# The first layer's down products with tokens standing and channels moving, summed by tokens and turned by VectorE

## The chip, the cores and the metric

The kernel runs on one core of one Trainium2 chip. The metric is the device time of one execution in microseconds (us). The engines of the core are named as in the profile: PE (TensorE, matmuls), PEld (its weight loads), DVE (VectorE), ACT (ScalarE), POOL (GpSimd) and SP (SyncE, which here only issues DMAs). A matmul has a standing operand of 128x128, loaded into the array ahead of it, and a moving one of up to 512 columns that streams past; its sums are kept in PSUM, 8 banks of 128x512 float32.

## The reference

One layer of a decoder trunk over 512 tokens of 1024 channels, all float32: a half-step SwiGLU feed-forward layer, a mixer (a linear recurrence beside sliding-window attention), and a second feed-forward layer. The change touches the first feed-forward layer and the border to the mixer:

```python
def swiglu(x, w_gu, w_down):
    gate, up = jnp.split(x @ w_gu, 2, axis=-1)
    return (jax.nn.silu(gate) * up) @ w_down

x = x + 0.5 * rms_norm(swiglu(rms_norm(x, ffn1_pre_g[l]), ffn1_w_gu[l], ffn1_w_down[l]), ffn1_post_g[l])
y = hybrid_mixer(rms_norm(x, mix_pre_g[l]), w_in[l], ...)
```

The hidden width is 2816, which is 22 chunks of 128. The product with `w_down` (2816 x 1024) is the "down product"; the kernel calls its result y.

## The kernel before

**Precision.** Every float32 operand is split into a high part, rounded by ACT, and a low part, the difference, made by DVE. A product is three matmuls: high by high, high by low, low by high.

**Groups.** The first layer works through its 22 hidden chunks in groups (`GROUPS1`): 0 to 4 ("classic" products), then three groups of four and a last one of six. In groups 1 to 4 `octo` makes four hidden chunks with a seven-product scheme for 2x2 blocks of matrices (seven "forms" in place of eight block products); its result comes out by tokens, is turned by DVE in blocks of 32x32 (`turned`, line 961), written to HBM by four DMAs (line 965) and read back turned (line 1021, or line 1035 in the last group). While `octo` of one group runs, `seven_forms_of` fetches the group before and makes the seven forms of its hidden values, and `seven_down` then does that group's down product, again with seven forms. So the down products of groups 1, 2 and 3 go through `seven_down`; those of group 0 and of the last group are plain.

**The down products.** They come out with channels on the partitions, as the border to the mixer needs them. In `by_channels` (lines 1339 to 1347) a 128x128 block of `w_down` stands and half of the tokens, 256 columns, move: 24 matmuls a form. The plain products (`product`, lines 506 to 508) let a block of `w_down` stand and all 512 tokens move.

**Sums of the groups.** Partial sums of y are kept in HBM (`in_hbm`, shown as yp_a). Group 0 writes them (line 1416), and each form of `seven_down` that finishes a block is copied out of PSUM by ACT (line 1113) and added to HBM by accumulating DMAs from POOL's queue (line 1116). At the end SP reads y's eight parts back, one for each chunk c of 128 channels (`parts[c]`, lines 1380 and 1389).

**The end of the layer.** The last group's hidden chunks 16 to 19 come from `octo`, 20 and 21 from `quad` (line 881 is its matmul line, in 7 forms). Then eight plain products over six chunks follow, c = 0 to 7, the first two together. For c = 0 to 4 `Residual.chunk` (line 676) adds the product to `parts[c]` on DVE; ACT squares it, and POOL adds up the squares. The last three (`LATE`) go through `boundary`, in two halves of tokens: the products of the first half, `late` on DVE (line 692), squares on ACT, sums on DVE (lines 705, 709); then PE forms the mean square (`stats`, line 550), ACT and DVE invert its root (lines 556 to 560), PE spreads it (line 564), DVE scales y and adds it to x (lines 713, 717), ACT rounds the mixer's input (line 580), and only then can PE begin the mixer's first products (lines 524 and 525).

**What sets the order.** The schedule is manual: each engine, and each DMA queue, runs its instructions in the order in which the program is written. `Weights` feeds the weights. `load` has SP issue the next raw tile (one of five buffers, tag "raw"), `take` and `fill` keep up to four units rounded (ACT) and split (DVE) ahead of the product. When the last unit of a raw tile is split, the next load is issued; if `W.owed` holds something, that is run in the load's place. x itself, two of the five raw buffers, is lent to HBM during the layer (`lend`) and read back (`give_back`, line 1357, POOL's queue) when c = 3.

Of the kernel before, what the change touches and what calls it, by code (L numbers as in the profile page):

```python
# [15 lines left out]
P = 128  # L16
# [106 lines left out]
def tile_layer(ctx: ExitStack, tc: tile.TileContext, out: bass.AP, **ins: bass.AP):  # L123
# [671 lines left out]
    def like(t, x):  # L795

        return t.rearrange("p (a b) -> p a b", a=2) if len(x.shape) == 3 else t

    class Hidden:


        def __init__(self, name, nxt):
            self.name, self.nxt, self.hs, self.g, self.u = name, nxt, {}, {}, {}

# [12 lines left out]
        def split(self, f):  # L817
            us, n = self.u.pop(f), f"{self.name}{f}"
            hh, hl = (spare.pop(), spare.pop()) if spare else (t2k(f"hh{n}", F32R), t2k(f"hl{n}", F32R))
            act.copy(hh, us)  # L820
            dve.tensor_sub(hl, us, hh.bitcast(F32))
            self.hs[f] = (hh, hl)

        def high(self, name, x):

            hh = t2k(f"hh{name}", F32R)
            act.copy(like(hh, x), x)
            self.forms[name] = hh, x

        def low(self, name):  # L830
# [3 lines left out]
            dve.tensor_sub(like(hl, x), x, like(hh.bitcast(F32), x))  # L834
# [171 lines left out]
        def seven_forms_of(self, f, h_hbm, at=(1, 2.5, 3.5, 4.5, 5.5, 6)):  # L1006
# [3 lines left out]
            def fetch():  # L1010
# [6 lines left out]
                z = wide(f"hx{self.name}{f}")  # L1017
                for s in range(2):
# [69 lines left out]
    def seven_down(hid, f, one, part, forms, ahead, beside={}, keep=False):  # L1088
# [7 lines left out]
        for n, (banks, form, blocks) in enumerate(((A, "a11", []), (Dd, "s3", [(1, 1)]), (B, "a12", [(0, 0)]), (A, "s2", [(1, 0)]),  # L1096
# [10 lines left out]
            for i in range(2 if form in (("s3", "s2") if keep else ("a12", "s3", "s2", "s4", "a22", "s1")) else 0):  # L1107
# [6 lines left out]
                for half, dh in blocks:  # L1114
                    o = part(half, dh, i)
                    pool.dma_start(o, st.rearrange("p (a b) -> p a b", a=2) if len(o.shape) == 3 else st, accum_op=ALU.add)  # L1116
# [203 lines left out]
    def masks():  # L1320
# [8 lines left out]
        dve.tensor_copy(up8f, upf)  # L1329
        return neg  # L1330
# [3 lines left out]
    in_hbm = [hbm.tile([P, 2, 2, T // 2], F32, name=f"yp_a{i}") for i in range(KD // 2)]  # L1334

    def in_halves(t):
        return t.rearrange("p (a b) -> p a b", a=2)

    def by_channels(banks, w, h, first):

        (hi, lo), (hh, hl_) = w, h
        for m in range(4):
            o, ms = banks[m // 2][:, HALF[m % 2]], slice(m * P, (m + 1) * P)
            for k in range(2):
                js = HALF[k]
                for i, (a, x) in enumerate(((hi, hh), (hi, hl_), (lo, hh))):
                    pe.matmul(o, a[:, k, ms], x[:, js], start=first and i + k + m % 2 == 0, stop=k == 1 and i == 2, skip_group_check=True)  # L1347
# [697 lines left out]
```

## Time and profile before

| | |
|---|---|
| three timed runs, median (lowest to highest) | 843.85 us (842.74 to 844.1) |
| the profiled execution, its own time | 842.55 us |
| its span in the trace, first to last instruction | 840.8 us |
| granted TensorE clock, mean | 0.999 |
| bytes moved by DMA over the span | 143.73 MB, mean 171 GB/s |
| accumulating DMAs of the first layer from POOL's queue (line 1116) | 42, of 256 KB each |

The stages that the change touches, by the trace (PE is busy through all of them):

| from, to (us) | on PE | DVE busy | DMA share |
|---|---|---|---|
| 58 to 78 | down products of group 0 | 19.20 of 20 | 0.82 |
| 116 to 292 | `octo` and `seven_down`, three times | 161.47 of 176 | 0.59, 0.79, 0.79 |
| 292 to 312 | `quad` | 13.87 of 20 | 1.09 |
| 312 to 332 | plain products c = 0 to 4 of the last group | 10.12 of 20 | 1.01 |
| 332 to 342 | late products, first half and on | 6.37 of 10 | 0.68 |
| 342 to 362 | border: norm, and the mixer's first products | 18.84 of 20 | 0.19 |

How to read the rows: times are us from the start of the span. A timeline row has the start, the time, the engine and line, the operation as out<-in, and in brackets how long the engine had been idle and what ended that. "SPq" is SP's DMA queue: its rows give the time that SP took to issue, not the time until the data have landed. "DMA share" is the mean busy share of the 16 DMA engines; queueing can take it above 1. Matmuls overlap, so one that "takes" 0.28 us can follow the last by 0.12; the chain of waits gives the time by which each one moves the end.

### The profile page before, as it was taken

How to read it: one execution, taken by the hardware profiler on the slowest of the kernel's cores; microseconds unless marked ns; L12 is line 12 of the kernel's file. 1: busy time of each engine (PE TensorE's matmuls, PEld its weight loads, DVE VectorE, ACT ScalarE, POOL GpSimd, SP SyncE). 2: the span in 40 equal slices, each digit the busy share in tenths (PEclk: the TensorE clock that was granted, in tenths of full speed). 3: DMA queues.
4: the chain of work that ended last, by engine and by line, in shares of the span. 5: the costliest groups of instructions: out<-in, count | busy, mean ns of one | idle time of the engine just before them, and what ended most of it. 6: DMA issues, size and time to landing. Idle time of an engine off the chain costs nothing.

```text
span 840.8 us, 12378 instructions
## 1 busy us (share of the span) xinstructions
PE 832.2 (99%) x4504; PEld 718.9 (85%) x4504; DVE 723.8 (86%) x1026; ACT 520.9 (62%) x821; POOL 162.6 (19%) x178
## 2 busy tenths in 40 slices
PE   9999999999999999999999999999999999999996
PEld 8988888988988998987788899888888888888885
DVE  4978999998989965879889589799999899898996
ACT  6646756666666655556797456536758667666562
POOL 2023000140320333304531052002004114032001
PEclk9999999999999999999999999999999999999999
DMA  7249429398595799323511131169439939769842
GB/s 252 77 128 347 135 79 318 80 251 267 123 255 186 167 261 331 93 62 108 157 51 51 51 105 47 50 129 290 179 106 232 317 92 257 253 149 258 305 140 101
DMA packets 123614, 143.73 MB, mean 171 GB/s; under 512 B 23897, under 2 KB 81569, under 8 KB 123041
## 3 DMA queue, kind: packets, MB, share of 16 engines
q1 hardware_dynamic: 109232, 111.86, 42.0%
q0 software_dynamic: 14176, 30.94, 17.0%
q8 instruction: 35, 0.57, 0.3%
q14 instruction: 27, 0.21, 0.1%
q10 hardware_dynamic: 144, 0.13, 0.0%
HBM read 100.45 MB, written 40.89 MB: 168 GB/s over the span
## 4 chain that ended last, share of the span: by engine, by line
PE 96%; DVE 2%; DMA 1%; SPq 0%; issue 0%; ACT 0%; DVEq 0%; ACTq 0%
PE aa L951 10%; PE ab L951 10%; PE db L951 5%; PE da L951 5%; PE yaa L1347 3%; PE bb L951 3%; PE ba L951 3%; PE yda L1347 2%; PE ya L506 2%; PE ya L507 2%; PE ya L508 2%; PE aa L881 1%; PE a_first L1206 1%; PE yab L1884 1%; PE yab L1885 1%; PE yab L1886 1%
## 5 line engine op out<-in xcount | busy, mean ns | idle before, releaser
L1116 POOL DMA_DIRECT2D yp_a<-stage x42 | 36.8, 1064 | 182.6 <-ACT stage L1113 158.8
L1116 POOL DMA_DIRECT2D yp_b<-stage x42 | 36.4, 1084 | 144.3 <-ACT stage L1113 117.8
L506 PE MATMUL ya<-hha,whi_ad 128*128 128x512 f32 x62 | 24.1, 389 | 0.0
L507 PE MATMUL ya<-hla,whi_ad 128*128 128x512 f32 x62 | 24.1, 389 | 0.0
L508 PE MATMUL ya<-hha,wlo_ad 128*128 128x512 f32 x62 | 24.1, 389 | 0.0
L686 POOL TENSOR_TENSOR acca_r<-acca_r,sq_r 128x512 f32<-128x512 f32 x6 | 8.1, 1357 | 61.7 <-ACT sq_r L536 61.7
L1900 POOL DMA_DIRECT2D yp_b<-stage x8 | 4.3, 548 | 67.1 <-ACT stage L1899 67.1
L524 PE MATMUL an<-xh_mx,whi_xl 128*128 128x256 f32 x64 | 15.9, 289 | 0.0
L525 PE MATMUL an<-xh_mx,wlo_xl 128*128 128x256 f32 x64 | 15.5, 283 | 0.0
L2003 POOL TENSOR_TENSOR last<-yp,grow 128x512 f32<-128x512 f32 x3 | 3.9, 1290 | 57.2 <-DVE yp L1993 57.2
L2000 ACT ACTIVATE ysq<-yp 128x512 f32<-128x512 f32 (+1 forms) x8 | 4.8, 606 | 16.2 <-DVE yp L1993 16.2
L506 PE MATMUL gt<-xh_mx,whi_gt 128*128 128x512 f32 x32 | 14.3, 445 | 0.0
L508 PEld LDWEIGHTS ya<-hha,wlo_ad 128*128 128x128 f32 x62 | 11.6, 188 | 2.4
L506 PEld LDWEIGHTS ya<-hha,whi_ad 128*128 128x128 f32 x62 | 11.6, 188 | 2.4
L507 PEld LDWEIGHTS ya<-hla,whi_ad 128*128 128x128 f32 x62 | 11.6, 188 | 2.4
L536 ACT ACTIVATE sq_r<-yp_a 128x256 f32<-128x256 f32 (+1 forms) x10 | 5.0, 502 | 12.9 <-DVE yp_a L676 5.9
L506 PE MATMUL pq<-xh_mx,whi_q 128*128 128x512 f32 x32 | 12.8, 399 | 0.0
L506 PE MATMUL pub<-xh_f,whi_bu 128*128 128x512 f32 x32 | 12.6, 395 | 0.0
L508 PE MATMUL gt<-xh_mx,wlo_gt 128*128 128x512 f32 x32 | 12.6, 394 | 0.0
L506 PE MATMUL pgb<-xh_f,whi_bg 128*128 128x512 f32 x32 | 12.6, 393 | 0.0
L507 PE MATMUL gt<-xl_mx,whi_gt 128*128 128x512 f32 x32 | 12.6, 392 | 0.0
L508 PE MATMUL pgb<-xh_f,wlo_bg 128*128 128x512 f32 x32 | 12.5, 390 | 0.0
(2014 smaller groups left out, 3468.8 us busy)
## 6 DMA issues: line engine op xcount, KB each, us to landing
yp_a<-stage POOLq DMA_DIRECT2D x50, 256.0 KB, 9.1
yp_b<-stage POOLq DMA_DIRECT2D x50, 256.0 KB, 9.0
h_a<-za SPq DMA_DIRECT2D x16, 256.0 KB
hxa<-h_a SPq DMA_DIRECT2D x16, 256.0 KB
h_b<-zb SPq DMA_DIRECT2D x16, 256.0 KB
hxb<-h_b SPq DMA_DIRECT2D x16, 256.0 KB
xn<-in_x SPq DMA_DIRECT2D x8, 256.0 KB
xT_hbm<-xT POOLq DMA_DIRECT2D x2, 1024.0 KB, 9.8
```

The source lines that it names most:

```text
L506: pe.matmul(ps, hi[:, k, :], xh, start=start, stop=False)
L507: pe.matmul(ps, hi[:, k, :], xl, start=False, stop=False)
L508: pe.matmul(ps, lo[:, k, :], xh, start=False, stop=stop)
L524: pe.matmul(ps[:, sl], hi[:, k, :], xh, start=k == 0 and not goes_on, stop=False, skip_group_check=True)
L525: pe.matmul(ps[:, sl], lo[:, k, :], xh, start=False, stop=False, skip_group_check=True)
L881: pe.matmul(o, w[:, k, js], x, start=first and i + j + k == 0, stop=k == 3 and i == 2, skip_group_check=True)
L951: pe.matmul(b[tb], x[:, blk], w[:, k, :], start=first and q + k + j == 0, stop=q + k == 2 and j == 2, skip_group_check=True)
L1116: pool.dma_start(o, st.rearrange("p (a b) -> p a b", a=2) if len(o.shape) == 3 else st, accum_op=ALU.add)
L1206: pe.matmul(banks[j][:, HALF[0]], ws[j][part][:, k, :], n1.xs[k][xpart][:, HALF[0]], start=k == 0 and part == xpart, stop=stop and k == KD ...
L1347: pe.matmul(o, a[:, k, ms], x[:, js], start=first and i + k + m % 2 == 0, stop=k == 1 and i == 2, skip_group_check=True)
L1884: pe.matmul(banks[i], hh[:, js], hi[:, k, :], start=first and k == 0, stop=False, skip_group_check=True)
L1885: pe.matmul(banks[i], hh[:, js], lo[:, k, :], start=False, stop=False, skip_group_check=True)
```

## The change

**Group 0.** Its `w_down` comes in two loads of 512 channels instead of four of 256. `first_down` computes y by tokens: a 128x128 block of the hidden values stands, 512 channels move, and four token blocks use four banks. Their copies go to HBM by rows (`rows_hbm`, shown as yr_a). `split` writes the hidden values of this group in another order of tokens (`in_blocks`).

**Groups 1 to 3.** `by_dealt_tokens` takes the place of `by_channels`: 12 matmuls of 512 columns a form instead of 24 of 256. `seven_forms_of` fetches each group by two larger DMAs and makes the forms from strided views (`dealt_halves`, `by_blocks`). In the last `seven_down` (`hold`) the form s1 isn't copied out: its two banks stay in PSUM (`held`).

**The end of the layer.** Since y is now summed by tokens, it has to be turned. The two places in `W.owed` read y's rows into two raw buffers (`read_rows`). `turn_sums(0)` turns the first 512 channels on DVE and writes them to HBM with four DMAs, and `read_sums` reads them back as `parts[0]` to `parts[3]`. `turn_sums(1)` comes when c = 1: it adds the held banks, turns, writes, and the other four parts are read back. `masks` moves from c = 0 to c = 2.

```diff
         if g == 0:
             for f in range(2, f1, 2):
                 add_gate_up(w1, f, "a")
+            for dh in range(2):
+                r = W.raw(lambda dh=dh: load_raw([ins["ffn1_w_down"][0, :f1 * P, HALF_D[dh]]], f1, T, f"ad0{dh}"))
+                for i in range(0, f1, 2):
+                    add_unit(r, lambda raw, i=i: raw[:, i:i + 2, :], 2, T, f"ad0{i}{dh}")
+            continue
...
+    def by_blocks(t, x):
+
+        if len(x.shape) == 3 and x.shape[1] == 2 * NB:
+            return t.rearrange("p (b q n) -> p q b n", b=2, n=32), x.rearrange("p q (b n) -> p q b n", b=2)
+        return like(t, x), x
...
-            act.copy(hh, us)
-            dve.tensor_sub(hl, us, hh.bitcast(F32))
+            if self.in_blocks:
+                act.copy(in_turn(hh), dealt(us))
+                dve.tensor_sub(in_turn(hl), dealt(us), in_turn(hh.bitcast(F32)))
+            else:
+                act.copy(hh, us)
+                dve.tensor_sub(hl, us, hh.bitcast(F32))
...
+                if dealt_halves:
+                    for s in range(2):
+                        own = z[:, 2 * s * T:2 * (s + 1) * T]
+                        sync.dma_start(own.rearrange("p (j n) -> p j n", j=2), h_hbm[2 * s * P:2 * (s + 1) * P].rearrange("(j p) n -> p j n", p=P))
+                        x[s, 0], x[s, 1] = (own.rearrange("p (q s m) -> p s q m", s=2, m=64)[:, h] for h in range(2))
+                    return
...
-            for i in range(2 if form in (("s3", "s2") if keep else ("a12", "s3", "s2", "s4", "a22", "s1")) else 0):
+            for i in range(2 if form in (("s3", "s2") if keep else ("a12", "s3", "s2", "s4", "a22") + (() if hold else ("s1",))) else 0):
...
+    def by_token_blocks(o, h, w, k, blk, start, stop):
+
+        (hh, hl_), (hi, lo) = h, w
+        for j, (x, a) in enumerate(((hh, hi), (hh, lo), (hl_, hi))):
+            pe.matmul(o, x[:, blk], a[:, k, :], start=start and j == 0, stop=stop and j == 2, skip_group_check=True)
+
+    def by_dealt_tokens(banks, w, h, first):
+
+        for i in range(2):
             for k in range(2):
-                js = HALF[k]
-                for i, (a, x) in enumerate(((hi, hh), (hi, hl_), (lo, hh))):
-                    pe.matmul(o, a[:, k, ms], x[:, js], start=first and i + k + m % 2 == 0, stop=k == 1 and i == 2, skip_group_check=True)
+                by_token_blocks(banks[i], h, w, k, slice((2 * i + k) * P, (2 * i + k + 1) * P), first and k == 0, k == 1)
...
+    def read_rows(dh):
+        t = wpool.tile([P, NB * T], F32, tag="raw", name=f"rows_a{dh}", bufs=NRAW)
+        row_sums[dh] = [t[:, tb * T:(tb + 1) * T] for tb in range(NB)]
+        for tb in range(NB):
+            sync.dma_start(row_sums[dh][tb], rows_hbm[tb, dh])
+
+    def turn_sums(dh):
+        z = wide(f"zy{dh}")
+        for tb in range(NB):
+            if dh:
+                dve.tensor_add(row_sums[dh][tb], row_sums[dh][tb], held[tb % 2])
+            dve.transpose(z.rearrange("p (j b n) -> p b j n", n=32, b=NB)[:, tb], row_sums[dh][tb].rearrange("p (j n) -> p j n", n=32))
+        for i in range(4):
+            sync.dma_start(turned_hbm[dh][:, i * P:(i + 1) * P].rearrange("(j a) n -> a j n", a=32), z[32 * i:32 * (i + 1)].rearrange("p (j n) -> p j n", n=P))
+
+    def read_sums(cs):
+        for c in cs:
+            parts[c] = t2k(f"yp_a{c}")
+            sync.dma_start(parts[c], turned_hbm[c // 4][(c % 4) * P:(c % 4 + 1) * P])
+
+    def first_down(hs):
+
+        for dh in range(2):
+            ybanks = [bank(f"ya0{dh}{tb}") for tb in range(NB)]
+            for f in range(len(hs)):
+                if f % 2 == 0:
+                    w = W.take()
+                for tb in range(NB):
+                    by_token_blocks(ybanks[tb], hs[f], w, f % 2, slice(tb * P, (tb + 1) * P), f == 0, f == len(hs) - 1)
...
+            for tb in range(NB):
+                st = t2k("stage")
+                act.activation(st, ybanks[tb], AF.Copy, scale=-1.0 if dh else 1.0)
+                pool.dma_start(rows_hbm[tb, dh], st)
...
             if g > 1:
-                seven_down(hid, before, by_channels, lambda half, dh, i: in_hbm[2 * dh + i][:, half], hid.forms, AHEAD - 1)
+                held = seven_down(hid, before, by_dealt_tokens, lambda half, dh, i: rows_hbm[2 * half + i, dh], hid.forms, AHEAD - 1, hold=f1 == FC)[1, 1]
             if f1 == FC:
-                W.owed = [lambda: None] * 2
+                W.owed = [lambda: read_rows(0), lambda: read_rows(1)]
...
+        res = Residual("r1", lambda c: half_g[:, c:c + 1])
+        turn_sums(0)
+        read_sums(range(4))
         for c in range(KD):
-            if f1 == FC and c == 0:
+            if c == 0:
                 load_gates()
...
-            if f1 == FC and c == 1:
+            if c == 1:
+                turn_sums(1)
+                read_sums(range(4, KD))
                 preload(AF.Sqrt)
+            if c == 2:
+                neg, upf = masks()
+            if c == 4:
+                dve.tensor_copy(up8f, upf)
```

How the order of the instructions moves at the end of the layer:

DVE before, from the last two instructions of `quad` (line 891, which split its hidden values) to the first `chunk` additions (line 676, c = 0 and 1); wlo_ad are low parts of the last group's `w_down`, up is a mask:

```order
L891 TENSOR_TENSOR hla_3075<-g1a_3085,hha_3074 128x2x4x32
L891 TENSOR_TENSOR hla_3077<-g1a_3085,hha_3076 128x2x4x32
L1329 CAST up_590<-upf 128x512
L215 TENSOR_TENSOR wlo_ad_0_3284<-raw_ad__3210,whi_ad_0_3283 128x768
L215 TENSOR_TENSOR wlo_ad_1_3346<-raw_ad__3210,whi_ad_1_3345 128x768
L676 TENSOR_TENSOR yp_a_3322<-ya_3354,yp_a_3322 128x512
L676 TENSOR_TENSOR yp_a_3324<-ya_3355,yp_a_3324 128x512
```

DVE in the changed kernel, the same stretch (line 908 is what 891 was, line 681 what 676 was; rows_a are y's rows, zy the turned tile, yaa the held banks):

```order
L908 TENSOR_TENSOR hla_2797<-g1a_2805,hha_2796 128x2x4x32
L1383 STREAM_TRANSPOSE zy_3052<-rows_a_2807 128x16x32 x4
L215 TENSOR_TENSOR wlo_ad_0_3014<-raw_ad__2940,whi_ad_0_3013 128x768
L215 TENSOR_TENSOR wlo_ad_1_3076<-raw_ad__2940,whi_ad_1_3075 128x768
L681 TENSOR_TENSOR yp_a_3061<-ya_3084,yp_a_3061 128x512
L1382 TENSOR_TENSOR rows_a_2870<-rows_a_2870,yaa_2609 128x512
L1383 STREAM_TRANSPOSE zy_3124<-rows_a_2870 128x16x32
L1382 TENSOR_TENSOR rows_a_2870<-rows_a_2870,yaa_2610 128x512
L1383 STREAM_TRANSPOSE zy_3124<-rows_a_2870 128x16x32
```

Four turns now stand ahead of the addition of c = 0, and four additions with four turns behind it and ahead of that of c = 1.

SP's queue in the changed kernel, from the last read of the first turned half to the mixer's weights (yt_a is the turned y in HBM, yp_a its parts read back, raw_xl and raw_kv the mixer's first raw weights):

```order
L1390 DMA yp_a_3067<-yt_a_599 128x512
L1332 DMA gates_raw<-in_w_rg 64x4x64 x2
L1332 DMA gates_raw<-in_w_ig 64x4x64 x2
L175 DMA raw_xl__3079<-in_w_in 128x8x256
L1385 DMA yt_a_600<-zy_3124 32x16x128 x4
L1390 DMA yp_a_3137<-yt_a_600 128x512
L1390 DMA yp_a_3139<-yt_a_600 128x512
L1390 DMA yp_a_3141<-yt_a_600 128x512
L1390 DMA yp_a_3143<-yt_a_600 128x512
L175 DMA raw_xl__3191<-in_w_in 128x8x256
L175 DMA raw_kv<-in_w_in 128x8x256
```

Before, the second of the two raw_xl loads stood behind plain reads of yp_a; now it stands behind the write of the second turned half and the reads that need that write. The write and the four reads of the first half stand in the same way ahead of the first raw_xl.

ACT in the changed kernel, in the same stretch (line 541 is the squaring, line 536 before; line 210 rounds weights):

```order
L541 ACTIVATE sq_r_3216<-yp_a_3067 128x512
L210 CAST whi_xl_1_3221<-raw_xl__3079 128x1024
L541 ACTIVATE sq_r_3244<-yp_a_3137 128x512
L210 CAST whi_xl_0_3250<-raw_xl__3191 128x1024
L541 ACTIVATE sq_r_3291<-yp_a_3139 128x256
```

The order of ACT is what it was before; the cast of the second raw_xl stands ahead of the squares of the late chunks, and its tile is now the one that SP issues later.

More of the change, by code (lines that the diff above doesn't have):

```diff
@@ L1086, in last_chunks, with seven_down @@
             return [self.hs.pop(c) for c in range(f, f + 6)]
-    def seven_down(hid, f, one, part, forms, ahead, beside={}, keep=False):
+    def seven_down(hid, f, one, part, forms, ahead, beside={}, keep=False, hold=False):
         free = [r_tile] + 3 * [acc_tile]
@@ L1407, in tile_layer @@
             b = pair_banks[c] if c < 2 else product(W.take(), xs, name=f"ya{g}{c}")
-            if g == 0 and c in (0, 1, 3, 4):
-                (n1.sums if c in (0, 3) else n1.lows)(2 + c // 3)
-            if g == 0 and c == 3:
-                lend(x_tiles)
-                W.load(2)
-            if g == 0:
-                st = t2k("stage")
-                act.activation(st, b, AF.Copy, scale=-1.0 if c >= KD // 2 else 1.0)
-                pool.dma_start(in_hbm[c // 2][:, :, c % 2], in_halves(st))
-            else:
-                res.chunk(c, b, parts[c])
+            res.chunk(c, b, parts[c])
     mx = Next("mx", "mix_pre_g")
```

57 lines of the change are left out of this document (27 added, 30 removed).

## The prediction

> **What bounds the kernel now.** First the page: busy times and the chain of waits.
>
> ```profile
> span 840.8 us, 12378 instructions
> PE 832.2 (99%) x4504; PEld 718.9 (85%) x4504; DVE 723.8 (86%) x1026; ACT 520.9 (62%) x821; POOL 162.6 (19%) x178
> PE 96%; DVE 2%; DMA 1%; SPq 0%; issue 0%; ACT 0%; DVEq 0%; ACTq 0%
> ```
>
> PE sets the end almost everywhere: a matmul saved is time saved, as long as no other engine becomes late. So there are two questions, what PE's work costs now and after, and whether PE can be made to wait. For the first, the chain of waits in order of time, a `seven_down` of each layer with what follows it:
>
> ```profile
> 155.01 2.87 PE yaa L1347 x24
> 172.28 2.88 PE yaa L1347 x24
> 175.16 5.47 PE aa L951 x24
> 616.48 5.44 PE ab L951 x24
> 640.96 5.44 PE ab L951 x24
> ```
>
> In the first layer (line 1347) the seven forms run from 155.01 to 175.16, 20.15 us. In the second, which already lets tokens stand and channels move, they run from 616.48 + 5.44 = 621.92 to 640.96, 19.04 us. For the second I read where PE must wait for others: the end of the layer and the border behind it, on PE, DVE, ACT and SP in turn (chain and timelines).
>
> ```profile
> 308.96 2.88 PE aa L881 x24
> 341.82 0.50 PE L550 MATMUL rms_r<-mean_d,accb_r 128*128 128x1 f32 x4
> 346.09 0.28 PE L524 MATMUL an<-xh_mx,whi_xl 128*128 128x256 f32 x1
> ```
>
> ```profile
> 315.53 0.76 DVE L891 TENSOR_TENSOR hla<-g1a,hha 128x256 fp32r<-128x256 f32 x2 [0.47 <-ACT hha L888]
> 319.39 1.37 DVE L676 TENSOR_TENSOR yp_a<-ya,yp_a 128x512 f32<-128x512 f32 x2 [1.02 <-PE ya L508]
> 332.31 0.69 DVE L676 TENSOR_TENSOR yp_a<-ya,yp_a 128x512 f32<-128x512 f32 x1 [2.25 <-PE ya L508]
> 339.84 0.43 DVE L709 TENSOR_TENSOR accb_r<-accb_r,sq_r 128x256 f32<-128x256 f32 x1 [0.53 <-ACT sq_r L536]
> ```
>
> ```profile
> 312.39 0.84 ACT L210 CAST whi_ad<-raw_ad__3210 128x768 fp32r<-128x768 f32 x1 [3.91 <-DMA raw_ad__3210<-in_ffn_w_down]
> 333.57 1.03 ACT L210 CAST whi_xl<-raw_xl__3440 128x1024 fp32r<-128x1024 f32 x1
> 345.38 1.63 ACT L580 ACTIVATE xh_mx<-xT,cols 128x256 fp32r<-128x256 f32 x3 [0.65 <-DVE xT L717]
> ```
>
> `quad` ends on PE at 308.96 + 2.88 = 311.84. DVE has the last low part of its hidden values at 315.53 + 0.76 = 316.29. At each `chunk` addition (L676) DVE waits for PE alone; y's parts have long landed. The sum of squares of the first half is ready at 339.84 + 0.43 = 340.27, and PE takes it at 341.82: only 1.55 us to spare. From there PE has 27 matmuls left until the mixer's first product at 346.09, whose input ACT begins to make at 345.38. This border has almost no slack: **what makes the sum of squares late by more than 1.55 us, PE loses.**
>
> **The change part by part.** *PE.* 504 matmuls of 256 columns (three groups of 168) become 252 of 512. By the two `seven_down`s above that saves 20.15 - 19.04 = 1.11 us a group, 3.3 in all, and `quad` then ends at 308.5. Group 0 keeps its number and size of matmuls, 96 of 512 columns: nothing.
>
> *Dealt forms.* The copies and subtractions on strided views can be read where the kernel already makes such views:
>
> ```profile
> L648 ACT CAST b2h_a<-xb_a x4: 621/622/623, 32.4 to 68.7; 128x512 fp32r<-128x512 f32 x4
> L827 ACT CAST hha<-hxa x9: 611/612/613, 131.3 to 266.9; 128x512 fp32r<-128x512 f32 x9
> L659 DVE TENSOR_TENSOR b2l_a<-xb_a,b2h_a x4: 684/686/687, 34.1 to 71.5; 128x512 fp32r<-128x512 f32 x4
> L834 DVE TENSOR_TENSOR hla<-hxa,hha x9: 677/692/694, 134.3 to 281.8; 128x512 fp32r<-128x512 f32 x9
> ```
>
> Line 648 and 659 are strided, 827 and 834 plain: 10 ns more and 6 ns less, so nothing. The larger fetches, group 0's four copies in a row and its moved weight units are work of the same amount with units rounded four ahead; PE's 20 us there hide it. Were that cover gone, a late cast of 1 us would cost 1 us.
>
> *The turn of y.* This is the part that counts. By the order, DVE turns the first half after the last instruction of `quad` (the one that ends at 316.29 before). SP writes it to HBM, reads it back when all four writes have landed, and DVE needs the first read for the addition of c = 0. Only behind that addition stand `turn_sums(1)`, a second write, a second read, and then the addition of c = 4. DVE runs in order, so the two trips to HBM follow one another. Their prices are in the second layer's last group, where the same transfers run with the queues free:
>
> ```profile
> 796.80 2.82 SPq L965 DMA_DIRECT2D h_b<-zb  x4
> 802.98 1.76 SPq L1035 DMA_DIRECT2D hxb<-h_b  x4
> 805.70 1.27 ACT L820 CAST hhb<-hxb 128x512 fp32r<-128x512 f32 x2 [0.38 <-DMA hxb<-h_b]
> 270.74 1.29 DVE L961 STREAM_TRANSPOSE za<-u2a 128x512 f32<-128x512 f32 x2
> ```
>
> From the first write (796.80) to the first read that may start (802.98) 6.2 us; from there to the reader (805.70) 2.7. Two turns take 1.29, four 2.6, one 0.64. An addition takes 0.69 (L676). Then, on the clock of the profile:
>
> - the last low part of `quad`: 316.29 - 3.3 = 313.0. ACT's cast of raw_ad (at 312.39 above) stands ahead of it. Its load now sits in SP's queue behind eight reads of rows, which wait for accumulations. Bounds: 1.5 us sooner, since PE's part of this wait is only 311.84 + silu, product and split; 4 us later, as long as that wait was (3.91). I take +0.5: 313.5
> - four turns, 2.6: 316.1. Write, 6.2: 322.3. Read, 2.7: 325.0. Addition of c = 0, 0.7: 325.7 (before: 320)
> - `turn_sums(1)`, four pairs of an addition and a turn that needs it, 4 x (0.69 + 0.64) = 5.3: 331.0
> - write, 6.2: 337.2. Read, 2.7: 339.9, addition of c = 4 (before: 332.31). From that row to the sum of squares took 340.27 - 332.31 = 8.0: 347.9.
>
> That alone is 347.9 - 341.82 = 6.1 us late. But the order of SP's queue adds a wait. The second raw_xl is issued after the four reads, 337.2 + 1.8 = 339.0 (the 1.76 of line 1035 above). ACT's cast of it stands ahead of the squares of the late chunks, and DVE's low part ahead of their additions. What a 1 MB load takes until ACT has it:
>
> ```profile
> 559.65 0.46 SPq L175 DMA_DIRECT2D raw_bd<-in_ffn_w_down  x1
> L210 ACT CAST whi_bd<-raw_bd x2: 1032/1040/1047, 565.1 to 566.5; 128x1024 fp32r<-128x1024 f32 x2
> xT<-xT_hbm POOLq DMA_DIRECT2D x2, 1024.0 KB, 7.3
> ```
>
> 565.1 - 559.65 = 5.4 with little else under way, 7.3 for x's 1 MB loads under contention. Those loads of x now come at about the same time (POOL issues them after the squares of c = 2), so the delay by sharing lies between 0 and 1.9; I take 0.9. The cast starts at 339.0 + 5.4 + 0.9 = 345.3. From that cast to the sum of squares took 340.27 - 333.57 = 6.7: 352.0, which is **10.2 us late**. The 3.3 us saved are in this sum already: PE only arrives sooner and waits.
>
> *The restart.* PE then stands still for over 10 us. What that does to its clock can be seen at the end of the span:
>
> ```profile
> 834.00:837.00 3.00, 0.23 (x2) 0.03 (x1) 2.68 (x10) 1.31 (x5) 0.00 (x0) 1.00 0.01 1
> 837.00:841.00 4.00, 0.00 (x0) 0.00 (x0) 0.34 (x1) 0.00 (x0) 0.00 (x0) 0.68 0.37 133
> ```
>
> PE's last matmul is at 834.2 (0.23 us busy in the first row), and in the second its granted clock falls to a mean of 0.68: it drops within a few us of idling. How long it stays low once PE works again no row shows. At worst the 27 matmuls behind the wait, 27 x 0.12 = 3.3 us by the pace of line 1347 (2.88 for 24), take twice as long; at best nothing. I take the middle, 1.7. The Trainium skill ("TensorE: Matmul & The Clock Gate", "Part 1: The HAM clock gate") states that about 3.4 us of idling halves the clock and about as long a busy stretch restores it. By that the cost here would be an estimated 1.7 us, half of 3.4; the trace agrees with its first half (0.68 above), and no row shows the second.
>
> Sum: 10.2 + 1.7 = 11.9 us. Made against the span, 840.8 + 11.9 = 852.7; the profiled execution took 842.55 in all and the runs' median is 843.85, 1.3 more, so 843.85 + 11.9 = **855.7 us**.
>
> The moved `masks` cost nothing: POOL's part comes behind what it waits 18.10 us for now, and DVE's copy of the mask lies in DVE's wait for c = 4. Were that cover gone, they would cost the work of one addition, 0.7.
>
> ```profile
> 322.85 1.30 POOL L686 TENSOR_TENSOR acca_r<-acca_r,sq_r 128x512 f32<-128x512 f32 x1 [18.10 <-ACT sq_r L536]
> ```
>
> **The rivals.** *Only the trips, not the weights* (20%): the second raw_xl lands in time because its issue isn't held up, and the addition of c = 4 is the last link: 6.1 + 1.7 = 7.8, 851.6 us. For it: raw_xl has free buffers. Against: SP's queue is issued in order.
>
> *quad's hidden values late too* (10%): raw_ad lands 4 us later instead of 0.5, and PE waits for the hidden values of chunk 20 as well. PE needs them 24 matmuls of 0.227 after `quad`, at 311.84 + 5.44 = 317.28, and has 1.0 us to spare. Everything moves by 3.5: 859 us. For it: raw_ad already landed late (3.91 us of waiting). Against: four accumulations fewer run at that moment, since s1 is held.
>
> *Faster* (7%): both trips are hidden, and the 3.3 us stay: 840.5 us. It decides at the addition of c = 4: that must come at 332.31 - 3.3 + 1.55 = 330.6 at the latest, while even without the sharing, and with raw_ad 1.5 us early, I get 339.9 - 2.0 = 337.9. Each trip would have to take 5.3 us instead of 8.9. For it: nothing but that this transfer's price is from another place.
>
> *Partly hidden* (3%): 0 to 2 us of loss, about 844. It needs trips of 6 us.
>
> If the matmuls with tokens standing don't run at the second layer's pace, the first link starts up to 3.3 us later and the sum grows by as much.
>
> **How the numbers follow.** The forecast holds 60%. Its own unknowns are 0.5 (-2.0, +3.5), 0.9 (-0.9, +1.0) and 1.7 (-1.7, +1.6). The low end of the range takes in the rival without the weights with its unknowns low: 6.1 - 2.0 = 4.1, 848. The high end, 860, takes in the late raw_ad. Less than 2 in 10 is outside. What can be told from no change is about 0.2%, 1.7 us. Slower 91%, same 2%, faster 7%.
>
> **What would show it.** In the changed kernel's profile: `seven_down` of the first layer at 2.72 a form; DVE idle some 7 us ahead of the first line 681 (325.0 less 316.1, less the low parts between), ended by a DMA of yp_a; line 681 of c = 4 at about 340; ACT waiting for raw_xl ahead of the late squares; PE idle for some 10 us ahead of line 555 (550 before), and slower matmuls right behind. It would be wrong if DVE didn't wait there, or if line 555 came before 342.

## The result, and the profile after

| | before | changed |
|---|---|---|
| median (lowest to highest), same chip | 843.98 us (842.74 to 844.16) | 864.97 us (863.75 to 866.78) |
| ratio to before, 95% interval | | 1.0254 [1.0232, 1.0275] |
| span of the profiled execution | 840.8 us | 865.1 us |
| granted TensorE clock, mean | 0.999 | 0.984 |

The kernel became 21.0 us slower, where 11.9 were forecast; 864.97 lies above the range. The profiled execution of the changed kernel is the slowest of its four (866.78), so its trace has 3.3 us more loss than the median.

The page of the changed kernel; its line numbers are higher by 5 here (550 is 555, 676 is 681):

```profile
span 865.1 us, 11869 instructions
PE 836.4 (97%) x4252; PEld 710.1 (82%) x4252; DVE 731.1 (85%) x1034; ACT 518.2 (60%) x815; POOL 159.0 (18%) x174
```

PE's busy time rose by 4.2 us, with 252 matmuls fewer: matmuls at a low clock take longer (below, 13 in 3 us at a granted clock of 0.50, 27 at 1.00). The rest of the loss is idle time, in two places. PE's timeline around `quad` and the border:

```profile
310.09 0.40 PE L511 MATMUL ya<-hha,whi_ad 128*128 128x512 f32 x1
317.54 0.50 PE L511 MATMUL ya<-hha,whi_ad 128*128 128x512 f32 x1 [1.82 <-ACT hha L905]
362.64 1.01 PE L555 MATMUL rms_r<-mean_d,accb_r 128*128 128x1 f32 x4 [17.83 <-DVE accb_r L714]
369.88 0.28 PE L529 MATMUL an<-xh_mx,whi_xl 128*128 128x256 f32 x1
```

`quad` ended at 310.09 (before: 311.84). At 317.54 PE had waited 1.82 us for the hidden values of chunk 20, and at 362.64 17.83 us for the sum of squares. Line 555 comes 20.8 us later than line 550 did (341.82), the mixer's first product 23.8 us later (369.88 against 346.09). What PE waits for is on DVE, ACT, SP and POOL (timelines):

```profile
317.52 0.76 DVE L908 TENSOR_TENSOR hla<-g1a,hha 128x256 fp32r<-128x256 f32 x2 [0.47 <-ACT hha L905]
318.20 2.48 DVE L1383 STREAM_TRANSPOSE zy<-rows_a 128x512 f32<-128x512 f32 x4
329.76 0.69 DVE L681 TENSOR_TENSOR yp_a<-ya,yp_a 128x512 f32<-128x512 f32 x1 [7.37 <-DMA yp_a<-yt_a]
345.14 0.68 DVE L681 TENSOR_TENSOR yp_a<-ya,yp_a 128x512 f32<-128x512 f32 x1
```

```profile
314.38 0.83 ACT L210 CAST whi_ad<-raw_ad__2940 128x768 fp32r<-128x768 f32 x1 [7.50 <-DMA raw_ad__2940<-in_ffn_w_down]
356.41 1.04 ACT L210 CAST whi_xl<-raw_xl__3191 128x1024 fp32r<-128x1024 f32 x1 [9.92 <-DMA raw_xl__3191<-in_w_in]
```

```profile
307.52 0.38 SPq L175 DMA_DIRECT2D raw_ad__2940<-in_ffn_w_down  x1
320.71 2.83 SPq L1385 DMA_DIRECT2D yt_a<-zy  x4
326.94 1.77 SPq L1390 DMA_DIRECT2D yp_a<-yt_a  x4
335.78 2.84 SPq L1385 DMA_DIRECT2D yt_a<-zy  x4
342.11 1.78 SPq L1390 DMA_DIRECT2D yp_a<-yt_a  x4
343.93 0.44 SPq L175 DMA_DIRECT2D raw_xl__3191<-in_w_in  x1
```

```profile
344.08 1.17 POOL L1420 DMA_DIRECT2D xT<-xT_hbm  x2
```

The chain is the one that was forecast, link by link: the late raw_ad (ACT waits 7.50 us), the turn, the first trip (320.71 to 326.94 to 329.76), the second trip (335.78 to 342.11), and only then the second raw_xl (343.93), for which ACT waits 9.92 us. Two links are far longer than forecast. The first turn starts at 318.20 instead of 313.5, because raw_ad was issued only at 307.52 and ACT had it at 314.38. And from the issue of raw_xl to its cast it takes 356.41 - 343.93 = 12.5 us instead of 6.3, with x's two loads issued right beside it at 344.08.

### The profile page after: what moved, and what is told of

It reads as the page before. It is cut to its first block, busy times and chain, and to the rows that moved or that the text cites. A ratio compares the mean times of both kernels' runs of the same rounds, so it can differ in the third digit from the quotient of the medians.

```text
span 865.1 us, 11869 instructions
## 1 busy us (share of the span) xinstructions
PE 836.4 (97%) x4252; PEld 710.1 (82%) x4252; DVE 731.1 (85%) x1034; ACT 518.2 (60%) x815; POOL 159.0 (18%) x174
## 2 busy tenths in 40 slices
DMA packets 124699, 146.84 MB, mean 170 GB/s; under 512 B 23960, under 2 KB 78560, under 8 KB 124128
## 4 chain that ended last, share of the span: by engine, by line
PE 49%; DVE 6%; ACT 1%; DMA 1%; issue 1%; SPq 0%; DVEq 0%; ACTq 0%
PE ab L968 9%; PE db L968 4%; PE bb L968 3%; PE yab L1941 1%; PE yab L1942 1%; PE yab L1940 1%; PE mn L529 1%; PE an L529 1%; PE pq L511 1%; PE an L530 1%; PE mn L530 1%; PE gt L511 1%; PE pq L513 1%; PE pq L512 1%; PE mn L536 1%
## 5 line engine op out<-in xcount | busy, mean ns | idle before, releaser
L1139 POOL DMA_DIRECT2D yr_a<-stage x38 | 33.3, 1004 | 183.6 <-ACT stage L1136 157.2
L555 PE MATMUL rms_r<-mean_d,accb_r 128*128 128x1 f32 x16 | 2.5, 261 | 17.8 <-DVE accb_r L714 17.8
L555 PEld LDWEIGHTS rms_r<-mean_d,accb_r 128*128 128x128 f32 x16 | 2.5, 224 | 18.0 <-DVE accb_r L714 18.0
L511 PE MATMUL ya<-hha,whi_ad 128*128 128x512 f32 x30 | 12.3, 411 | 1.8 <-ACT hha L905 1.8
L512 PE MATMUL gt<-xl_mx,whi_gt 128*128 128x512 f32 x32 | 12.5, 392 | 0.0
L513 PE MATMUL pq<-xh_mx,wlo_q 128*128 128x512 f32 x32 | 12.5, 390 | 0.0
L513 PE MATMUL pgb<-xh_f,wlo_bg 128*128 128x512 f32 x32 | 12.5, 390 | 0.0
L512 PE MATMUL pq<-xl_mx,whi_q 128*128 128x512 f32 x32 | 12.5, 390 | 0.0
L513 PE MATMUL pub<-xh_f,wlo_bu 128*128 128x512 f32 x32 | 12.5, 390 | 0.0
L512 PE MATMUL pub<-xl_f,whi_bu 128*128 128x512 f32 x32 | 12.5, 390 | 0.0
```

The costliest lines, as they stand in the source:

```text
L511: pe.matmul(ps, hi[:, k, :], xh, start=start, stop=False)
L512: pe.matmul(ps, hi[:, k, :], xl, start=False, stop=False)
L513: pe.matmul(ps, lo[:, k, :], xh, start=False, stop=stop)
L1139: pool.dma_start(o, st, accum_op=ALU.add)
```

## The experiments

All ratios are to the kernel before on the same chip, with their 95% intervals. A difference in us to the changed kernel is one between medians taken on different chips; the medians of the kernel before lay between 842.95 and 843.98 us there, so such a difference is good to about 1 us.

### Is all of the loss behind the turn?

**e4_no_turn.** y's sums are read back untransposed:

```diff
-                W.owed = [lambda: read_rows(0), lambda: read_rows(1)]
+                W.owed = [lambda: None] * 2
...
-        turn_sums(0)
-        read_sums(range(4))
+        read_plain(range(5))
...
-                turn_sums(1)
-                read_sums(range(4, KD))
+                read_plain(range(5, KD))
```

> The changed products alone: tokens stand and 512 channels move in the first layer, but the sums are read back as they are, in the places where the kernel before read them; the turns, the trips and the held pair's addition are left out, so y's values are not the reference's. Theory: all of the loss is behind the turn, and 3.3 us of PE time are saved less 1.5 for weights that came late in the first seven_down: 842 (841 to 843). Rival (the changed forms themselves, or late weights, delay the border too): 846 or more.

840.45 us, ratio 0.9967 [0.9955, 0.9979]. The products alone are worth 2.5 us, somewhat more than the 1.8 expected, and everything that was lost is lost by the turn (the reads of the rows, the turns and the trips together). In the trace of this run PE reaches line 555 without a wait, and the addition of c = 4 waits for PE only:

```profile
330.40 0.69 DVE L681 TENSOR_TENSOR yp_a<-ya,yp_a 128x512 f32<-128x512 f32 x1 [1.82 <-PE ya L513]
```

Why not 3.3 us? In the changed kernel the second and third `seven_down` of the first layer take the forecast 19.04 us, but the first takes 20.2 (155.50 to 175.70), as long as before, and PE leaves group 0 already 0.5 us later (79.34 against 78.85). In that first one DVE's low parts come late (DVE's timeline, then PE's):

```profile
165.80 1.21 DVE L322 TENSOR_TENSOR wlo_adt__1595<-raw_axd__1371,whi_adt__1594 128x1024 fp32r<-128x1024 f32 x1
166.93 0.68 DVE L851 TENSOR_TENSOR hls<-s4a,hhs 128x512 fp32r<-128x512 f32 x1
```

```profile
167.07 0.50 PE L1360 MATMUL yea<-wlo_adt__1595,hhs 128*128 128x512 f32 x1
167.68 0.50 PE L1360 MATMUL yea<-whi_adt__1594,hls 128*128 128x512 f32 x1
```

Each of these matmuls starts 0.06 to 0.07 us after the part it needs is done (165.80 + 1.21 = 167.01, 166.93 + 0.68 = 167.61). Why DVE is late there no run asked.

### The links of the chain, one at a time

**e1_ad_first** puts the two loads of raw_ad ahead of the eight reads of rows:

```diff
-                W.owed = [lambda: read_rows(0), lambda: read_rows(1)]
+                W.owed = [W.load, W.load, lambda: read_rows(0), lambda: read_rows(1)]
```

> The changed kernel with one queue order undone: the two loads of raw_ad stand ahead of the eight reads of rows again. Theory (three delays in a row: late raw_ad, two trips one after the other, late raw_xl): quad's last low part comes at 313.5 instead of 318.2 and all behind it moves with it, 4.7 us less than the changed kernel's 865.0, so about 860. Rival (the DMA engines are full at that time, and what raw_ad gains the rows lose): the turns start as late as now, 865 +- 1.

859.21 us, 1.0192 [1.0177, 1.0208]: 5.8 us less, 5.2 by the ratios. First SP's row of the kernel before, where raw_ad was issued at 298.37, not 307.52; then, of this run, ACT's cast of raw_ad and DVE's first turn:

```profile
298.37 0.47 SPq L175 DMA_DIRECT2D raw_ad__3210<-in_ffn_w_down  x1
```

```profile
306.37 0.83 ACT L210 CAST whi_ad<-raw_ad__2807 128x768 fp32r<-128x768 f32 x1 [0.89 <-DMA raw_ad__2807<-in_ffn_w_down]
```

```profile
311.64 2.48 DVE L1383 STREAM_TRANSPOSE zy<-rows_a 128x512 f32<-128x512 f32 x4
```

The turn comes 6.6 us earlier than in the changed kernel, and the rows, now read later, don't hold it up: the place in SP's queue was the cause, not the bytes.

**e2_xl_early** issues the second raw_xl ahead of the second turn's write:

```diff
             if c == 1:
+                W.load()
+                W.owed = [lambda: None]
                 turn_sums(1)
```

> The changed kernel with one load moved: the second raw_xl is issued ahead of the second turn and its write, right behind the first raw_xl (332.7 us instead of 343.9). Theory: it lands before the second trip is over, the addition of c = 4 at 345.1 becomes the last link, and the sum of squares is ready 8.0 us behind it, at 353.1 instead of 362.6: 9.5 us less, about 855.5. Rival (not the order but the DMA engines' load makes it late, x's reload above all): less than 5 us, 860 or more. Rival 2 (the load doesn't matter, only the trips): 865.

858.53 us, 1.0184 [1.0169, 1.0199]: 6.4 less, between the theory's 9.5 and the first rival's "less than 5". In the profiled executions, from which the 9.5 came, the spans differ by 8.1 (857.0 against 865.1). Line 555 comes within 1 us of the theory's time, and ACT no longer waits for the load:

```profile
346.54 1.03 ACT L210 CAST whi_xl<-raw_xl__3124 128x1024 fp32r<-128x1024 f32 x1
```

```profile
353.92 1.01 PE L555 MATMUL rms_r<-mean_d,accb_r 128*128 128x1 f32 x4 [10.12 <-DVE accb_r L714]
```

**e8_ad_and_xl** has both edits.

> The two orders of e1_ad_first and e2_xl_early together: raw_ad ahead of the rows, the second raw_xl ahead of the second turn. Theory (the delays stand one behind the other in one chain, so the gains add up): in e2_xl_early the last links are the addition of c = 4 at 345.3 and line 555 at 353.9; both come 5.5 us earlier, as the first turn did in e1_ad_first (311.6 against 317.2), 1.9% less 0.6%: about 853. Rival (both gains come from the same relief of the DMA engines, and don't add up): 857 to 859.

853.76 us, 1.0126 [1.0112, 1.014]. The gains of the two were 0.62% and 0.70%, both together give 1.28%: they add up, so the links stand one behind the other.

**e3_both_turns** takes the second turn right behind the first, so that the trips overlap:

```diff
         turn_sums(0)
-        read_sums(range(4))
+        turn_sums(1)
+        read_sums(range(KD))
```

> The changed kernel with the second turn right behind the first, ahead of the first addition: the two trips to HBM overlap. Theory: the second half's writes start at 326 instead of 335.8, its reads at 332, the second raw_xl at about 338 instead of 343.9 with a part of its contention left: 6 to 10 us less, 855 to 859. Rival (the trips are no link of the chain, only the load's contention with x's reload is): within 2 us of 865.

856.61 us, 1.0161 [1.0144, 1.0178]: 8.4 less, as the theory had it. The trips one behind the other were a link, but this run doesn't price them alone: with the trips joined, the second raw_xl is issued earlier too, at 336.14 instead of 343.93.

**e7_x_later** moves x's reload behind the last addition:

```diff
             if c == 3:
                 split_gates()
-                x_tiles[:] = give_back()
...
             res.chunk(c, b, parts[c])
+        x_tiles[:] = give_back()
```

> The changed kernel with x's reload (two loads of 1 MB on POOL's queue) issued behind the last addition instead of beside the second raw_xl. Theory (the second raw_xl takes 12.4 us because 3 MB share the DMA engines): POOL issues it at about 349, raw_xl lands some 3 us earlier, 862; x itself lands by 360 and isn't missed. Rival (raw_xl's 12.4 us come from its place in SP's queue alone): 865. Rival 2 (x becomes the last link): 866 or more.

859.13 us, 1.0188 [1.0172, 1.0204]: 5.8 less, twice what was expected. The second raw_xl on SP's queue, and its cast on ACT:

```profile
343.36 0.44 SPq L175 DMA_DIRECT2D raw_xl__3187<-in_w_in  x1
```

```profile
349.85 1.04 ACT L210 CAST whi_xl<-raw_xl__3187 128x1024 fp32r<-128x1024 f32 x1 [3.90 <-DMA raw_xl__3187<-in_w_in]
```

Issued at the same point, it takes 349.85 - 343.36 = 6.5 us, not 12.5, with raw_kv behind it on SP's queue in both. So all of the 6 us above the forecast came from the two loads of x on POOL's queue.

### The restart of PE

**e6_warm** fills 15 us of PE's wait with matmuls whose result nobody reads:

```diff
+    def keep_warm(x):
+        b = bank("warm_a")
+        for i in range(125):
+            pe.matmul(b[:, HALF[0]], x[:, :P], x[:, HALF[0]], start=i == 0, stop=i == 124)
...
```

> The changed kernel with 125 matmuls of 256 columns, that compute nothing used, ahead of line 555 in PE's wait (15 of its 17.8 us). Theory (the matmuls behind the wait run at half the granted clock because PE stood still): 3 us less, 862. Rival (the 7.4 us from line 555 to the mixer's first product, against 4.3 before, are waits for others): 865.

865.49 us, 1.0266 [1.0252, 1.028]: nothing gained. But the filling ended 1.50 us before line 555, and the clock fell after all (PE's timeline; then windows: PE, PEld, DVE, ACT, POOL busy, granted clock, DMA share, GB/s):

```profile
361.90 0.61 PE L555 MATMUL rms_r<-mean_d,accb_r 128*128 128x1 f32 x4 [1.50 <-DVE accb_r L714]
368.03 0.28 PE L529 MATMUL an<-xh_mx,whi_xl 128*128 128x256 f32 x1
```

```profile
364.00:367.00 3.00, 3.00 (x13) 2.82 (x14) 2.56 (x8) 1.04 (x3) 2.26 (x2) 0.50 0.08 19
```

**e10_warm_all** has 145 of these matmuls.

> As e6_warm, with 145 matmuls instead of 125: in e6_warm the filling ended 1.5 us before line 555 and the granted clock fell after all. Theory: PE now passes into line 555 without a pause, from there to the mixer's first product it takes about 4.3 us as before, not 7.4; less up to 1 us by which the filling runs past the wait, 862 to 863. Rival (the stretch behind line 555 waits for ACT and DVE, whatever the clock): 865 or more.

862.92 us, 1.0232 [1.0216, 1.0247]: about 2 us less than the changed kernel. The same two views:

```profile
361.66 0.61 PE L555 MATMUL rms_r<-mean_d,accb_r 128*128 128x1 f32 x4 [0.30 <-DVE accb_r L714]
366.25 0.28 PE L529 MATMUL an<-xh_mx,whi_xl 128*128 128x256 f32 x1
```

```profile
364.00:367.00 3.00, 3.00 (x27) 2.98 (x26) 3.00 (x9) 1.78 (x4) 2.68 (x3) 1.00 0.12 35
```

From line 555 to the mixer's first product it takes 4.6 us at clock 1.00, 6.1 in e6_warm, 7.2 in the changed kernel (369.88 - 362.64), 4.3 before. The restart costs 7.2 - 4.3 = 2.9 to 3.0 us, and nearly all of it is the clock.

### An order that gives the loss back?

**e5_early** joins the three: raw_ad ahead of the rows, the first turn ahead of `quad`'s last low part, the second right behind it, raw_xl ahead of the second trip (`write_sums` is the writing half of `turn_sums`).

```diff
-                W.owed = [lambda: read_rows(0), lambda: read_rows(1)]
+                W.owed = [W.load, W.load, lambda: read_rows(0), lambda: read_rows(1)]
...
-            xs = hid.last_chunks(f0, h_hbm[f0], {})
+            xs = hid.last_chunks(f0, h_hbm[f0], {6: lambda: (turn_sums(0), write_sums(0))})
...
+        load_gates()
+        read_sums(range(4))
+        turn_sums(1)
         for c in range(KD):
             if c == 1:
+                write_sums(1)
+                W.load()
...
```

> The changed kernel with the whole border put in another order: raw_ad ahead of the rows, the first turn ahead of quad's last low part, the second turn right behind that part, the gates' loads and both raw_xl ahead of the second trip's reads. Theory: the first half is read back at about 321, the second at about 329, the addition of c = 4 comes by 331, the sum of squares is in time, PE doesn't wait, and what stays is the gain of e4_no_turn: 840.5 (840 to 842), faster than the kernel before. Rival 1 (the rows land later than 310, or eight more transfers and the loads slow one another): 844 to 850. Rival 2 (turning ahead of the low part makes quad's hidden values late, deadline 315.5): 1 to 3 us of stall at the fifth pair, 843 or more.

847.88 us, 1.0054 [1.0041, 1.0067]: 17 us of the 21 are back, but not all. SP's queue shows where the rest goes:

```profile
313.39 2.83 SPq L1389 DMA_DIRECT2D yt_a<-zy  x4
320.01 1.89 SPq L1394 DMA_DIRECT2D yp_a<-yt_a  x4
322.00 0.38 SPq L175 DMA_DIRECT2D raw_xl__3088<-in_w_in  x1
322.49 6.30 SPq L1389 DMA_DIRECT2D yt_a<-zy  x4
333.68 1.77 SPq L1394 DMA_DIRECT2D yp_a<-yt_a  x4
```

The second write, right behind 1 MB of raw_xl, takes 11.2 us until its reads may start, where the first, issued at 313.39, took 6.6. What the Trainium skill says ("DMA: Bandwidth & Descriptors", "Queues, rings and completion order"), that each DMA engine takes up a queue's pieces in their order, agrees with this.

**e9_reordered** puts small transfers ahead of big ones: first raw_xl and gates into SP's idle time ahead of the first write, the second raw_xl behind the second write, x's reload last.

```diff
+            def first_turn():
+                W.load()
+                W.owed = [lambda: None]
+                load_gates()
+                turn_sums(0)
+                write_sums(0)
...
+                write_sums(1)
+                W.load()
+                W.owed = [lambda: None]
                 read_sums(range(4, KD))
...
+            if c == KD - LATE:
+                split_gates()
...
+        x_tiles[:] = give_back()
```

> e5_early put in another order, because its second write (issued at 322.5, landed at 333.6) stood in SP's queue behind 1 MB of raw_xl: the first raw_xl and the gates' loads ahead of the first write (SP is idle from 309 to 313 there), the second raw_xl behind the second write, x's reload behind the last addition, the gates' cast behind the fourth. Theory (each queue hands its transfers over in order, so a small write behind a big load waits for all of it): the second write lands by 329, the addition of c = 4 comes at 331 to 332.5 instead of 337.1, and PE's wait ahead of line 555 is under 2 us: 841 to 842.5, a little faster than the kernel before. Rival (it isn't the order but the bytes: 4 MB more in this stretch make whatever is last late): 845 to 848.

846.36 us, 1.0035 [1.0025, 1.0045], at the rival's end. The second write was issued at 323.02 and its reads at 330.68, 7.7 us later, not 11.2:

```profile
323.02 3.55 SPq L1389 DMA_DIRECT2D yt_a<-zy  x4
330.68 1.97 SPq L1394 DMA_DIRECT2D yp_a<-yt_a  x4
```

```profile
334.04 0.69 DVE L681 TENSOR_TENSOR yp_a<-ya,yp_a 128x512 f32<-128x512 f32 x1 [0.97 <-DMA yp_a<-yt_a]
```

```profile
342.14 0.60 PE L555 MATMUL rms_r<-mean_d,accb_r 128*128 128x1 f32 x4 [2.12 <-DVE accb_r L714]
348.03 0.28 PE L529 MATMUL an<-xh_mx,whi_xl 128*128 128x256 f32 x1
```

**e11_pool_reads** is e9_reordered with both trips' reads on POOL's queue, nothing between the two writes, and the reads of the second half placed at c = 3. Against e9_reordered:

```diff
-            sync.dma_start(parts[c], turned_hbm[c // 4][(c % 4) * P:(c % 4 + 1) * P])
+            pool.dma_start(parts[c], turned_hbm[c // 4][(c % 4) * P:(c % 4 + 1) * P])
...
         turn_sums(1)
+        write_sums(1)
         for c in range(KD):
             if c == 1:
-                write_sums(1)
                 W.load()
                 W.owed = [lambda: None]
+            if c == 3:
                 read_sums(range(4, KD))
```

> e9_reordered with the reads of both trips on POOL's queue, and the second write and the second raw_xl behind the first write on SP's queue with nothing between that waits. In e9_reordered the second write was issued at 323.0 only (behind the first reads), landed at 330.6, and its reads stood behind 1 MB of raw_xl. Theory: the second write is issued at 320.4 and lands by 327.5, its reads come at 330 on a queue of their own, the addition of c = 4 at 331 instead of 334.0, PE waits under 1 us ahead of line 555: 841 to 842.5, faster than the kernel before. Rival (the bytes in this stretch set it, not the queue they stand in): 845 to 848, as e9_reordered.

854.28 us, 1.0132 [1.0115, 1.0149]: worse than e9_reordered, and a miss. POOL, which does its instructions in order, issued the second half's reads only behind its sums of squares, and the first half's reads took until 327.4 beside the writes and raw_xl:

```profile
320.85 2.22 POOL L1394 DMA_DIRECT2D yp_a<-yt_a  x4 [23.29 <-DMA yt_a<-zy]
335.45 2.18 POOL L1394 DMA_DIRECT2D yp_a<-yt_a  x4
```

**e12_writes_first** has, against e9_reordered, both writes ahead of all reads, on SP's queue.

```diff
-        read_sums(range(4))
         turn_sums(1)
+        write_sums(1)
+        read_sums(range(KD))
         for c in range(KD):
             if c == 1:
-                write_sums(1)
                 W.load()
                 W.owed = [lambda: None]
-                read_sums(range(4, KD))
...
```

> e9_reordered with both writes of the trips ahead of all reads, and the second raw_xl behind them, all on SP's queue. Theory: the second write goes out at 320.4, into the stretch from 320 to 325 in which the DMA engines were busy only 0.58 of the time in e9_reordered, lands by 327; its reads land by 330.5 with nothing big ahead of them; the second raw_xl lands at 333.5, as late as it may be. The addition of c = 4 comes at 331, PE's wait ahead of line 555 (2.12 us there) is under 0.5: 841 to 843, 3 to 5 us below e9_reordered and not slower than the kernel before. Rival (the bytes of this stretch set it): as e9_reordered, 845 to 847.

849.34 us, 1.0072 [1.006, 1.0084], a miss as well. The first addition now came at 329.63, all additions and squares behind it in a row, and c = 4 at 338.72:

```profile
329.63 1.31 DVE L681 TENSOR_TENSOR yp_a<-ya,yp_a 128x512 f32<-128x512 f32 x2 [7.27 <-DMA yp_a<-yt_a]
338.72 0.68 DVE L681 TENSOR_TENSOR yp_a<-ya,yp_a 128x512 f32<-128x512 f32 x1
```

Does a bound that the forecast left out stand behind all four? Windows of the kernel before (the last three figures of a row are the granted clock, the DMA share and GB/s):

```profile
310.00:320.00 10.00, 10.00 (x53) 8.58 (x52) 7.08 (x13) 4.19 (x8) 0.00 (x0) 1.00 1.09 328
320.00:330.00 10.00, 10.00 (x46) 8.29 (x45) 4.96 (x7) 6.56 (x11) 5.23 (x6) 1.00 0.92 299
330.00:340.00 10.00, 10.00 (x77) 9.61 (x76) 5.64 (x10) 3.35 (x6) 2.70 (x2) 1.00 0.90 325
```

The 16 DMA engines were 0.90 to 1.09 busy in this stretch already. The change adds 4 MB to it: 2 MB of rows read, 2 MB written and 2 MB read back turned, in place of 2 MB of y's parts; four accumulations of 256 KB fall away (the page has 146.84 MB moved, 143.73 before). At 300 to 330 GB/s 3.1 MB are an estimated 9 to 10 us of work for all 16. That these bytes are the last bound is argued from these rows and not shown: a run with fewer bytes in the same order wasn't made, and the trace of e9_reordered speaks in part against it (windows):

```profile
320.00:325.00 5.00, 5.00 (x24) 4.14 (x23) 3.01 (x5) 0.37 (x1) 0.00 (x0) 1.00 0.58 172
340.00:345.00 5.00, 2.88 (x17) 2.59 (x16) 3.38 (x9) 2.39 (x7) 1.19 (x2) 0.85 1.06 397
345.00:350.00 5.00, 5.00 (x36) 4.94 (x35) 4.60 (x11) 2.73 (x6) 2.37 (x3) 0.81 0.87 284
```

The DMA engines had room there from 320 to 325 (0.58), and line 555 came only 0.3 us later than in the kernel before (342.14 against 341.82). Most of what this execution lost by then was lost behind it: PE had waited 2.12 us, its clock fell, and the mixer's first product (348.03) came 5.9 us after line 555 instead of 4.3. The eleven runs fit this: the fastest, 843.51 us, has the granted clock 0.999, the six with 0.996 or less took 845.37 to 847.86. Whether e9_reordered without that pause would match the kernel before, no run asked.

The four orders traded one late transfer for another, and the best one (e9_reordered) leaves 0.35%: by its median no version that turns the sums ran faster than the kernel before.

## Why the prediction was wrong

The direction and the chain were right, each waiting engine as forecast: DVE for y, ACT for raw_xl, PE ahead of line 555, then slow matmuls. Three terms of the sum were too small. By the steps of the prediction, in the profiled executions:

| step | forecast | measured |
|---|---|---|
| `seven_down`s save, `quad` ends earlier by | 3.3 | 1.8 |
| last low part of `quad`, first turn starts | 313.5 | 318.20 |
| four turns | 2.6 | 2.48 |
| write / read, first trip | 6.2 / 2.7 | 6.23 / 2.82 |
| `turn_sums(1)` | 5.3 | 5.4 (from 330.37) |
| write, second trip | 6.2 | 6.33 |
| second raw_xl issued | 339.0 | 343.93 |
| its load until the cast | 6.3 | 12.5 |
| from that cast to line 555 | 6.7 | 6.2 |
| line 555 later than before by | 10.2 | 20.8 |
| restart | 1.7 | 3.0 |

- **"the last low part of `quad`" with "I take +0.5"** failed: the low part ended at 318.28, 5.3 us behind the 313.0 without a delay, where the bound was 4. The wait of 3.91 us was taken as a measure of how much later a load could come, and PE's saving of 3.3 us was taken off a cast that waited for a load and not for PE. In the kernel before raw_ad took 14.0 us from its issue (298.37) to its cast (312.39). Behind the reads, which wait for their accumulations, it was issued 9.15 us later and took 6.9, so the cast came 2.0 us later than before, where the forecast had it 2.8 us earlier. With the load first again, in e1_ad_first, the turn starts at 311.64: its place in the queue cost 6.6 us in the traces, and 5.2 to 5.8 by the medians.
- The condition of the rival "quad's hidden values late too" came with it, and PE waited 1.82 us at the fifth pair; that didn't move the end by itself, since PE waited later anyway. The rival's 859 us had this link, but not the load of raw_xl.
- **"the delay by sharing lies between 0 and 1.9"** failed most: it was 6 us. The bound was what x's own loads took in the kernel before (7.3 us), and raw_xl's MB was then added to theirs without a price. Here x's two loads, issued just after raw_xl, took 8.0 and 10.2 us and landed before it. e7_x_later shows it. The 5.4 us of the sum were read in a stretch (559.60 to 565.10) in which the DMA engines were 0.96 busy, not "with little else under way".
- **"I take the middle, 1.7"** for the restart: 3.0, near the upper end (3.3). e10_warm_all shows it. The estimate of 1.7 us that the prediction sets beside it falls short by as much: from 362.64 to 369.87, over 7 us, the granted clock was 0.54 on the mean.
- In the traces the forecast is 11.9 us short (20.8 + 3.0 against 10.2 + 1.7): 4.9 by the time at which raw_xl is issued, 6.2 by its load, less 0.5 for the step behind it, and 1.3 by the restart.
- The rival "only the trips" is refuted by e2_xl_early and e8_ad_and_xl: the load cost 6 us more than the trips. "Faster" and "partly hidden" needed trips of 5 to 6 us; they took 9.
- The prices of the turn and of both trips, read from the second layer, were right to 0.2 us.

## What to carry to other kernels

What a reader sees of a load is when it lands. When something that waits is put into a queue ahead of it, work out the time of its new issue, and then what will run beside it until it has landed; the wait that it had before tells neither. Here an issue 9.15 us later came to a cast 2.0 us later, and the same 1 MB took 6.5 or 12.5 us by what ran beside it. The order of loads, writes and turns was worth 17 to 18 of the 21 us. The saving of 2.5 us on PE came with 3 MB more to move, to a border where PE had 1.55 us to spare and the DMA engines were 0.9 to 1.1 busy, and in none of the ten orders that were run with the turn did it pay. A pause of PE that is left has to be priced with the clock behind it.

## What the runs showed of the hardware

A short pause of PE can be followed by half the clock. In the changed kernel the pause of 1.82 us ahead of 317.54 was (windows):

```profile
318.00:321.00 3.00, 3.00 (x8) 2.36 (x8) 3.00 (x6) 0.53 (x1) 0.00 (x0) 0.53 0.00 0
```

After a pause of 1.64 us at the same place in e2_xl_early the clock stayed at 1.00:

```profile
316.60:318.60 2.00, 2.00 (x8) 1.46 (x9) 2.00 (x5) 0.94 (x2) 0.00 (x0) 1.00 0.00 0
```

In the traces of all these versions PE makes eleven pauses of 1.3 to 2.2 us between 40 and 820 us. Six were followed by a granted clock of 0.50 for some 3 us: 1.82 here, 1.50 and 1.85 in e6_warm, 1.84 in e11_pool_reads, 1.88 in e7_x_later and 2.12 in e9_reordered. Five were not: 1.35 in e6_warm, 1.40 and 2.06 in e10_warm_all, 1.64 and 1.81 in e2_xl_early. So the length alone doesn't decide it; what does, the runs don't tell.

The Trainium skill ("TensorE: Matmul & The Clock Gate", "HAM oscillation — how this bites in real kernels") has the rule to avoid idle gaps of PE above some 3.4 us; all eleven pauses are shorter, and six of them were followed by the low clock all the same.
